# Hybrid encoder layer on one core: the memory queries and the first half of the SSD gate of group one computed in the stage of seven products, the keys of group two one block later

## The chip, the core and the metric

The kernel runs on one core of a Trainium2 chip. TensorE (PE in the profile) multiplies 128x128 stationary tiles by moving tiles of up to 512 columns and writes to PSUM; VectorE (DVE), ScalarE (ACT) and GpSimd (POOL) work beside it, and SyncE (SP) issues the transfers. Each engine takes its own queue in order, and semaphores join them. The metric is the time of one execution in microseconds (us) on the device. Smaller is better.

## The reference

One layer of an encoder for 1280 tokens of width 2048 (256 of a prompt, 1024 of a sample), in fp32:

```python
hn = rms_norm(x, norm_g)
proj = hn @ w_in                       # 2048 -> 4896 columns
xbc, z_ssd, dt_raw, q, k, v, z_att, mq, z_mem = split_cols(proj, IN_SIZES)
xbc = silu(centred_dwconv(xbc))        # 1536 channels, five taps; then a two-way chunked SSD scan (y_f, y_b)
yg = (y_f + y_b + d_skip * xs) * silu(z_ssd)        # 1024 columns; an RMS norm over each half of 512
o_att = window_attention(rms(q), rms(k), v, sink) * silu(z_att)     # 8 heads, window 128
mq = rms_norm(mq.reshape(b, T, 4, 128), mq_norm_g)                  # memory queries, 512 columns
o_mem = softmax(mq @ mk.T * 128 ** -0.5) @ mv * silu(z_mem)         # 256 memory rows
return x + concat([rms(yg), o_att, o_mem]) @ w_out
```

The change touches two pieces of `proj`: the 512 columns `mq` and the first 512 of the 1024 columns `z_ssd` (the gate of the first SSD half). Both are computed for all tokens before and after; what differs is how, for the first half of the tokens.

## The kernel before, in words

**Tokens and precision.** The ten token tiles of 128 form two groups of five, group one (tiles 0 to 4) and group two (5 to 9). x is held turned, features by tokens. Every fp32 product is made of three matmuls on rounded parts: high by high, high by low, low by high. The weights are split on the chip: `wsplit` rounds a 128x512 piece on ACT (`wh`, line 201) and takes the rest on DVE (`wl`, line 202).

**Three forms of a projection block.** `block_tok` (lines 253 to 255) holds the tokens still and streams 512 weight columns: 16 steps of k, five tiles, three matmuls, 240 of 512 columns; its result has tokens on the partitions. `block_feat` (lines 288 to 290) holds 256 weight columns still and streams the tokens in halves of 320; its result is turned, features on the partitions. `block_pair` (lines 1197 to 1199) does a block of two by two (two halves of k, two of 128 columns each, two of 320 tokens) with seven products instead of eight, by Strassen's and Winograd's scheme: a unit covers 256 columns with 8 x 7 x 3 = 168 matmuls of 320 columns, and its result is turned. The sums of weight pieces that it needs are made by `weight_sums` on POOL (four per step of k, line 1169) and split like the weights; the seven accumulators are put together on DVE (`ev_seven`).

**Order of the stages.** Memory keys and values; attention queries of group one; then ten units of seven products for group one (`UNITS`, lines 1506 on): gates of attention and memory, and the convolution channels. Then ordinary blocks: keys, values and dt of group one (`kv`), memory queries (`mq`), the halves of the SSD gate (`z0`, `z1`, and during `z1` the x of group two is loaded). Then group two: five convolution blocks, its `kv`, the sixth convolution block, `q`, attention gate, `z0`, `z1`, `mq`, memory gate; then the output product, with a second stage of seven products at the end.

**Side work.** Attention, memory attention and the SSD scan are generators in two queues (lanes): lane 0 holds key and query preparation, `attn` and `mem_attn`, lane 1 `dt_prep`, `ssd_up`, `ssd_down`. After each k of a block, `pump` takes as many steps from each lane as `RATES` says (for `block_feat` half as many per k), so the rates set how densely side work lies between the block matmuls. `need` forces steps that are required at once. The order within an engine's queue is then fixed when the program is built.

**Side work that the change touches.** `mem_attn(t)` loads a tile of memory queries (line 704), squares it on ACT (707), sums on DVE, takes a reciprocal root on POOL, turns the four heads on PE (715) and splits them, then computes scores, a softmax, and passes the probabilities through a transfer of its own (`mprR`, line 749) to round them for the PE's turn (755). `attn` does the same with `lgR` (648) and `ppt` (658). `ssd_down(t)`, the backward pass of the scan, loads the partial y and the gate of each half (`zd`, line 1011), multiplies them (1031) and squares with a sum (1032). All small PSUM results share a ring of three buffers (`mix`).

**Sums of squares of x.** `x_stats` computes row statistics by ACT squares; for tiles 5, 6 and 7 this happens during the seven-product stage (`stage_stats`), for tiles 8 and 9 as a generator in lane 1.

Of the kernel before, what the change touches and what calls it, by code (L numbers as in the profile page):

```python
# [19 lines left out]
P = 128  # L20
# [22 lines left out]
def hymba_encoder_kernel(  # L43
# [62 lines left out]
    zT_d = [[dram([P, 4, 640], f"zT{c}_{g}") for g in range(2)] for c in range(2)]  # L106
    q_d = [dram([P, 512], f"q_{t}") for t in range(NT)]
    mq_d = [dram([P, 512], f"mq_{t}") for t in range(NT)]
    k_d = [dram([P, P], f"k_{t}") for t in range(NT)]
# [589 lines left out]
    def mem_attn(t):  # L699
# [4 lines left out]
        S.dma_start(q, mq_d[t])  # L704
        yield
        sq = w2("sq")
        A.activation(sq, q, AF.Square)
# [5 lines left out]
        ps = psum("pmq")  # L713
        for h in range(4):
            T.transpose(ps[:, h * P:(h + 1) * P].bitcast(F32R), qr[:, h * P:(h + 1) * P], identr)
# [280 lines left out]
    def ssd_down(t):  # L996
# [8 lines left out]
        for g in range(2):  # L1005
            c = slice(g * 512, (g + 1) * 512)

            y = mp.tile([P, 512], F32, tag="ya" if t % 2 else "rf", name="yd", bufs=2)
            S.dma_start(y, yp_d[t][:, c])
            z = mp.tile([P, 512], F32, tag="xs", name="zd", bufs=2)  # L1010
            S.dma_start(z, z_d[g][t])
# [257 lines left out]
    def ev_seven(kind, f0):  # L1269

        work, o = (conv_left, 2) if kind is None else (gate_left, 0)
# [35 lines left out]
    def gate_left(c, f0, rs):  # L1307
        th = []

        def tanhs():  # L1310
            for r in rs:
                th.append(ev.tile([P, 640], F32, tag="evt", name="th"))
                A.activation(th[-1], r[:, :640], AF.Tanh, scale=0.5)

        def last(i):
            V.scalar_tensor_tensor(out=th[i], in0=th[i], scalar=1.0, in1=rs[i][:, :640], op0=ALU.add, op1=ALU.mult)
            S.dma_start(zT_d[c][0][:, f0 + i, :], th[i])
        return [tanhs, lambda: last(0), lambda: last(1)]
# [27 lines left out]
    def x_stats(grp):  # L1346
        if grp == 0:
            yield from stats([(xrow(t), t) for t in range(5)],
                             lambda i: ev.tile([P, 512], F32, tag="evt" if i % 2 else "evu", name="xst"))
        else:  # L1350
            yield from stats([(xrow(t), t) for t in (8, 9)],
                             lambda i: mp.tile([P, 512], F32, tag="xs" if i % 2 else "ya", name="xst", bufs=2))
# [131 lines left out]
    units = [(i // 2, i % 2 * 2) if i < 4 else (None, 2 * (i - 4)) for i in UNITS]  # L1484
# [44 lines left out]
    queue(1, x_stats, [1])  # L1529
# [30 lines left out]
    for b in range(5):  # L1560
        feat("x", b, ev_conv(1, 2 * b), 1, extra=one_left)
    need(attn, range(4))
    kv_shift()
    run(block_tok(w_kv, 5, ev_dtkv(5)), RATES[1]["kv"], extra=one_left)
# [7 lines left out]

    run(block_tok(w_in_rows("q"), 5, ev_raw(q_d, 5)), RATES[1]["q"], extra=when_done(2, lambda: queue(1, ssd_up, range(4, 8))))
# [108 lines left out]
```

## Time and profile before

| | before |
|---|---|
| median of 3 runs | 1803.69 us (1802.4 to 1804.88) |
| profiled execution | 1804.15 us, of it 1802.4 us span from the first to the last instruction |
| PE busy | 1789.5 us (99%) |
| weight loads busy | 1600.9 us (89%) |
| DVE busy | 1211.0 us (67%) |
| ACT busy | 901.0 us (50%) |
| POOL busy | 457.4 us (25%) |

The times of a matmul in the profile are the time it spends in PE, which overlaps with the next; what a stream costs is seen from start to start, or from a stretch divided by its matmuls. "Idle before" is time in which an engine did nothing, put down to what ended it.

### The profile page before, as it was taken

How to read it: one execution, taken by the hardware profiler on the slowest of the kernel's cores; microseconds unless marked ns; L12 is line 12 of the kernel's file. 1: busy time of each engine (PE TensorE's matmuls, PEld its weight loads, DVE VectorE, ACT ScalarE, POOL GpSimd, SP SyncE). 2: the span in 40 equal slices, each digit the busy share in tenths (PEclk: the TensorE clock that was granted, in tenths of full speed). 3: DMA queues.
4: the chain of work that ended last, by engine and by line, in shares of the span. 5: the costliest groups of instructions: out<-in, count | busy, mean ns of one | idle time of the engine just before them, and what ended most of it. 6: DMA issues, size and time to landing. Idle time of an engine off the chain costs nothing.

```text
span 1802.4 us, 30786 instructions
## 1 busy us (share of the span) xinstructions
PE 1789.5 (99%) x10546; PEld 1600.9 (89%) x10546; DVE 1211.0 (67%) x2303; ACT 901.0 (50%) x1999; POOL 457.4 (25%) x772
## 2 busy tenths in 40 slices
PE   9999999999999999999999999999999999999999
PEld 8789999999887799999989988777888888889999
DVE  5595788877557878775755756556784654766665
ACT  6554455444445757464426645554483533543332
POOL 0105899961010000000000000001100000058775
PEclk9999999999999999999999999999999999999999
DMA  8654454447545655545436556567885664644442
GB/s 298 191 178 123 136 151 147 130 135 217 166 138 173 222 163 156 163 137 154 130 100 202 165 157 194 158 198 243 252 278 179 203 206 144 222 147 147 143 142 79
DMA packets 213293, 309.48 MB, mean 172 GB/s; under 512 B 20560, under 2 KB 92304, under 8 KB 213136
## 3 DMA queue, kind: packets, MB, share of 16 engines
q1 hardware_dynamic: 212992, 307.45, 55.1%
q8 instruction: 83, 1.36, 0.3%
q14 instruction: 74, 0.61, 0.1%
q10 hardware_dynamic: 144, 0.06, 0.0%
HBM read 231.12 MB, written 57.44 MB: 160 GB/s over the span
## 4 chain that ended last, share of the span: by engine, by line
PE 88%; issue 4%; DMA 4%; DVE 2%; ACT 1%; POOL 1%; SPq 0%; ACTq 0%; DVEq 0%; POOLq 0%
PE acc L253 13%; PE acc L255 12%; PE acc L254 12%; PE acc L1199 6%; PE acc L1197 6%; PE acc L1198 6%; PE acc L288 5%; PE acc L289 5%; PE acc L290 5%; PE accm L1198 2%; PE accm L1197 2%; PE accm L1199 2%; PE py L929 2%; PE po L668 1%; PE pmo L770 1%
## 5 line engine op out<-in xcount | busy, mean ns | idle before, releaser
L202 DVE TENSOR_TENSOR wl<-wraw,wh 128x512 fp32r<-128x512 f32 (+1 forms) x480 | 339.4, 709 | 279.4 <-ACT wh L201 271.4
L253 PE MATMUL acc<-wh,xH 128*128 128x512 f32 (+1 forms) x1248 | 480.6, 385 | 0.4 <-DVE dt_all L331 0.4
L254 PE MATMUL acc<-wl,xH 128*128 128x512 f32 (+1 forms) x1248 | 473.5, 379 | 0.9 <-DVE wl L202 0.8
L255 PE MATMUL acc<-wh,xL 128*128 128x512 f32 (+1 forms) x1248 | 472.7, 379 | 0.0
L201 ACT ACTIVATE wh<-wraw 128x512 fp32r<-128x512 f32 (+1 forms) x480 | 292.9, 614 | 355.0 <-PE acc L255 203.0
L253 PEld LDWEIGHTS acc<-wh,xH 128*128 128x128 f32 x1248 | 234.4, 188 | 44.3 <-issue 4.0
L254 PEld LDWEIGHTS acc<-wl,xH 128*128 128x128 f32 x1248 | 234.5, 188 | 44.1 <-DVE wl L202 3.7
L255 PEld LDWEIGHTS acc<-wh,xL 128*128 128x128 f32 x1248 | 234.3, 188 | 44.3 <-issue 1.1
L288 PE MATMUL acc<-xH,wh 128*128 128x320 f32 x640 | 202.8, 317 | 0.0
L289 PE MATMUL acc<-xL,wh 128*128 128x320 f32 x640 | 198.6, 310 | 0.0
L290 PE MATMUL acc<-xH,wl 128*128 128x320 f32 x640 | 198.0, 309 | 0.0
L202 DVE TENSOR_TENSOR sl<-ws,sh 128x384 fp32r<-128x384 f32 x144 | 100.0, 698 | 98.1 <-ACT sh L201 97.8
L201 ACT ACTIVATE sh<-ws 128x384 fp32r<-128x384 f32 x144 | 74.6, 523 | 181.8 <-POOL ws L1169 85.1
L1169 POOL TENSOR_TENSOR ws<-wraw 128x128 f32<-128x128 f32 x144 | 90.8, 631 | 200.3 <-DMA wraw<-in_w_in_pairs_dram 78.2
L289 PEld LDWEIGHTS acc<-xL,wh 128*128 128x128 f32 x640 | 120.2, 188 | 2.8 <-issue 2.4
L288 PEld LDWEIGHTS acc<-xH,wh 128*128 128x128 f32 x640 | 120.2, 188 | 2.2 <-issue 1.6
L290 PEld LDWEIGHTS acc<-xH,wl 128*128 128x128 f32 x640 | 120.2, 188 | 0.3 <-issue 0.2
L628 POOL COPY lg<-nsink 128x2 f32<-128x2 f32 x40 | 11.5, 288 | 412.1 <-DMA lgR<-lg 214.8
L357 DVE SCALAR_TENSOR_TENSOR c<-u,vec,c 128x638 f32<-128x638 f32 (+1 forms) x96 | 89.2, 930 | 12.2 <-ACT c L352 11.8
L1169 POOL TENSOR_TENSOR ws<-ws,wraw 128x128 f32<-128x128 f32 x144 | 96.7, 671 | 0.0
L1169 POOL TENSOR_TENSOR ws<-wraw,ws 128x128 f32<-128x128 f32 x144 | 92.9, 645 | 11.3
L1169 POOL TENSOR_TENSOR wraw<-wraw 128x128 f32<-128x128 f32 x144 | 89.7, 623 | 11.1
(426 smaller groups left out, 3592.1 us busy)
## 6 DMA issues: line engine op xcount, KB each, us to landing
wraw<-in_w_in_laid_dram SPq DMA_DIRECT2D x208, 256.0 KB, 2.9
wraw<-in_w_in_pairs_dram SPq DMA_DIRECT2D x80, 256.0 KB, 2.8
wraw<-in_w_out_laid_dram SPq DMA_DIRECT2D x64, 256.0 KB, 3.2
wraw<-in_w_out_pairs_dram SPq DMA_DIRECT2D x64, 256.0 KB, 2.8
rf<-ac SPq DMA_DIRECT2D x40, 256.0 KB, 3.7
rb<-ac SPq DMA_DIRECT2D x40, 256.0 KB, 4.0
lgR<-lg SPq DMA_DIRECT2D x48, 192.0 KB, 2.2
wraw<-in_w_mem_laid_dram SPq DMA_DIRECT2D x32, 256.0 KB, 4.6
```

The costliest lines, as they stand in the source:

```text
L201: a = A.activation(h, raw, AF.Copy)
L202: b = V.tensor_sub(l, raw, h.bitcast(F32))
L253: T.matmul(ps[t][:, :n], sh, h[:, :n], start=(k_ == 0), stop=False)
L254: T.matmul(ps[t][:, :n], sh, l[:, :n], start=False, stop=False)
L255: T.matmul(ps[t][:, :n], sl, h[:, :n], start=False, stop=(k_ == KT - 1))
L288: T.matmul(o, sh, cur["H", q][:, m, c], start=(k == 0), stop=False)
L289: T.matmul(o, sh, cur["L", q][:, m, c], start=False, stop=False)
L290: T.matmul(o, sl, cur["H", q][:, m, c], start=False, stop=(k == KT - 1))
L1169: G.tensor_tensor(out=o, in0=x, in1=y, op=op)
L1197: T.matmul(ps[p], h, xh, start=(k_ == 0), stop=False)
L1198: T.matmul(ps[p], h, xl, start=False, stop=False)
L1199: T.matmul(ps[p], l, xh, start=False, stop=(k_ == 7))
```

## The change

1. Group one's `mq` and `z0` blocks go. In their place come four units of seven products, so the stage has 14 units instead of 10. Two of them (`y0`, `y1`) make the gate of the first SSD half with the same end as the other gates (tanh and product), stored turned in `yT_d`; two (`m0`, `m1`) store raw memory queries turned in `mT_d`.
2. `mem_attn` of group one reads turned queries. It needs them turned for the scores and by tokens for the sum of squares, so it turns them first, squares what comes out, and splits the loaded tile directly.
3. `ssd_down` of tiles 0 to 4 reads the first half's gate turned, and turns it on PE into a PSUM tile before the product.
4. The sums of squares of tiles 8 and 9 move from lane 1 into the seven-product stage.
5. The keys of group two come after the sixth convolution block instead of before it. `mem_attn` of group one is queued before the `z1` block.
6. The rates are set anew.
7. The weights of the units are laid out for the new order by the host.

```diff
-RATES = ({'kv': (2.14, 1.0), 'mq': (2.57, 1.6), 'z0': (2.35, 1.7), 'z1': (2.35, 1.7)},
-         {'kv': (1.28, 1.5), 'x': (1.87, 1.85), 'q': (1.71, 2.5), 'za': (1.71, 2.5), 'z0': (1.66, 2.6), 'z1': (1.66, 2.65), 'mq': (1.66, 2.8), 'zm': (1.66, 2.85), 'o': (2.09, 1.9)})
+RATES = ({'kv': (2.14, 1.0), 'z1': (3.21, 1.6)},
+         {'kv': (1.5, 1.5), 'x': (2.25, 2.15), 'q': (2.35, 2.5), 'za': (2.19, 2.5), 'z0': (2.14, 2.6), 'z1': (2.03, 2.65), 'mq': (2.03, 2.8), 'zm': (2.03, 2.85), 'o': (2.09, 1.9)})
-UNITS = (0, 4, 1, 5, 2, 6, 7, 3, 8, 9)
+UNITS = (0, 8, 1, 9, 2, 10, 3, 11, 4, 12, 5, 13, 6, 7)
+PAIRS = ('za0', 'za1', 'zm0', 'zm1', 'y0', 'y1', 'm0', 'm1', 'x0', 'x1', 'x2', 'x3', 'x4', 'x5')
...
 def mem_attn(t):
-        S.dma_start(q, mq_d[t])
+        if grp == 0:
+            S.dma_start(hv(q, 4), mT_d[:, :, tc_])
+        else:
+            S.dma_start(q, mq_d[t])
         yield
+        def turned():
+            ps = psum("pmq")
+            for h in range(4):
+                T.transpose(ps[:, h * P:(h + 1) * P].bitcast(F32R), qr[:, h * P:(h + 1) * P], identr)
+            return ps
+        tok_ = turned() if grp == 0 else q
         sq = w2("sq")
-        A.activation(sq, q, AF.Square)
+        A.activation(sq, tok_, AF.Square)
...
-        ps = psum("pmq")
-        for h in range(4):
-            T.transpose(ps[:, h * P:(h + 1) * P].bitcast(F32R), qr[:, h * P:(h + 1) * P], identr)
+        feat_ = q if grp == 0 else turned()
-        A.activation(qh, ps, AF.Copy)
+        A.activation(qh, feat_, AF.Copy)
-        V.tensor_sub(ql, ps, qh.bitcast(F32))
+        V.tensor_sub(ql, feat_, qh.bitcast(F32))
...
 def ssd_down(t):
+            if g == 0 and t < 5:
+                z = mp.tile([P, 512], F32R, tag="xs", name="zd", bufs=2)
+                S.dma_start(hv(z.bitcast(F32), 4), yT_d[:, :, tok])
...
+            if g == 0 and t < 5:
+                zr, z = z, psum("pz")
+                for j in range(4):
+                    T.transpose(z[:, j * P:(j + 1) * P].bitcast(F32R), zr[:, j * P:(j + 1) * P], identr)
...
-        yield from stats([(mrow(i), 10 + i) for i in range(4)] + [(xrow(t), t) for t in (5, 6, 7)],
+        yield from stats([(mrow(i), 10 + i) for i in range(4)] + [(xrow(t), t) for t in range(5, 10)],
...
+    def turned_left(dst, f0, rs):
+        def store():
+            for i in range(2):
+                S.dma_start(dst[:, f0 + i, :], rs[i][:, :640])
+        return [store]
...
-    queue(1, x_stats, [1])
...
-    run(block_tok(w_in_rows("mq"), 5, ev_raw(mq_d, 0)), RATES[0]["mq"],
+    queue(0, mem_attn, range(5))
+    run(block_tok(w_in_rows("z1"), 5, ev_gate(1, 0)), RATES[0]["z1"], refill_x(1),
         extra=when_done(1, lambda: queue(1, ssd_up, range(4))))
-    queue(0, mem_attn, range(5))
-    tok("z0", w_in_rows("z0"), ev_gate(0, 0))
-    tok("z1", w_in_rows("z1"), ev_gate(1, 0), refill_x(1))
...
-    for b in range(5):
+    for b in range(6):
         feat("x", b, ev_conv(1, 2 * b), 1, extra=one_left)
...
     run(block_tok(w_kv, 5, ev_dtkv(5)), RATES[1]["kv"], ...)
...
-    feat("x", 5, ev_conv(1, 10), 1, extra=one_left)
```

More of the change, by code (lines that the diff above doesn't have):

```diff
@@ L1344, in stats, with x_stats @@
                 yield
[L1346 to L1352, printed above, removed]
+    def x_stats(_):
+        yield from stats([(xrow(t), t) for t in range(5)],
+                         lambda i: ev.tile([P, 512], F32, tag="evt" if i % 2 else "evu", name="xst"))
     def stage_stats():
-        yield from stats([(mrow(i), 10 + i) for i in range(4)] + [(xrow(t), t) for t in (5, 6, 7)],
+        yield from stats([(mrow(i), 10 + i) for i in range(4)] + [(xrow(t), t) for t in range(5, 10)],
                          lambda i: fin.tile([P, 512], F32, tag="xst", name="sst"), ahead=1, group=3)
@@ L1482, in hymba_encoder_kernel @@
         extra=lambda k: p_step(16 + k))
-    units = [(i // 2, i % 2 * 2) if i < 4 else (None, 2 * (i - 4)) for i in UNITS]
+    dests = (zT_d[0][0], zT_d[1][0], yT_d, mT_d)
+    units = [(dests[i // 2], i % 2 * 2) if i < 8 else (None, 2 * (i - 8)) for i in UNITS]
     squares = stage_stats()
@@ L1558, in one_left, with gate @@
             some_left()
-    for b in range(5):
+    for b in range(6):
         feat("x", b, ev_conv(1, 2 * b), 1, extra=one_left)
+    def gate(name, c, after=None):
+        for b in range(2):
+            feat(name, b, ev_gateT(c, 1, 2 * b), 1, after if b else None)
     need(attn, range(4))
     kv_shift()
-    run(block_tok(w_kv, 5, ev_dtkv(5)), RATES[1]["kv"], extra=one_left)
+    run(block_tok(w_kv, 5, ev_dtkv(5)), RATES[1]["kv"], extra=lambda k: some_left() if left else None)
     queue(0, k_prep, range(5, 10))
@@ L1567, in hymba_encoder_kernel @@
     queue(1, dt_prep, [5])
-    feat("x", 5, ev_conv(1, 10), 1, extra=one_left)
-    def gate(name, c, after=None):
-        for b in range(2):
-            feat(name, b, ev_gateT(c, 1, 2 * b), 1, after if b else None)
     run(block_tok(w_in_rows("q"), 5, ev_raw(q_d, 5)), RATES[1]["q"], extra=when_done(2, lambda: queue(1, ssd_up, range(4, 8))))
@@ L1653 @@
     at = {n: c for n, c, _ in _blocks()}
[L1654 to L1656 removed]
+    at.update({f"{n}{b}": at[s][256 * b:256 * b + 256] for n, s in (('y', 'z0'), ('m', 'mq')) for b in range(2)})
+    c = _np.concatenate([at[PAIRS[i]] for i in UNITS])
+    p = w[:, c].reshape(2, 8, P, len(UNITS), 2, P)
+    inputs['w_in_pairs'] = _np.stack([p[0, :, :, :, 0], p[1, :, :, :, 0], p[1, :, :, :, 1], p[0, :, :, :, 1]]).transpose(3, 1, 2, 0, 4).reshape(len(UNITS), 8, P, 512)
     inputs['w_mem_laid'] = _np.asarray(inputs['w_mem_kv'])[0].reshape(KT, P, 2, 512).transpose(2, 0, 1, 3)
```

16 lines of the change are left out of this document (8 added, 8 removed).

## The prediction, made before the result was known

> **What bounds the kernel now.** I read the page's first and fourth parts, then busy times by stretch, then PE's waits, and last single tiles.
>
> ```profile
> PE 1789.5 (99%) x10546; PEld 1600.9 (89%) x10546; DVE 1211.0 (67%) x2303; ACT 901.0 (50%) x1999; POOL 457.4 (25%) x772
> ...
> PE 88%; issue 4%; DMA 4%; DVE 2%; ACT 1%; POOL 1%; SPq 0%; ACTq 0%; DVEq 0%; POOLq 0%
> ```
>
> PE is busy for all but 13 us of the 1802.4 us span, and the chain that ended last is PE for 88%. Time can be won only by taking work off PE, and lost only by making PE wait. The stretches are stages: seven products for group one (151.9 to 399.2), keys, values and dt of group one up to 430.8, memory queries (to 491.5), first half of the SSD gate (to 554.7), second half (to 632.6), five convolution blocks and the keys of group two (to 862.8), its other projections (to 1257.2), the memory gate and the output blocks, of which the last (from 1545.8) is matmuls alone. Columns: stretch, length, then busy time and instructions of PE, PEld (weight loads), DVE, ACT and POOL, the clock, the DMA share and GB/s.
>
> ```profile
> core 0: us, PE busy (x) PEld busy (x) DVE busy (x) ACT busy (x) POOL busy (x), PEclk, DMA share, GB/s
> 151.90:399.20 247.30, 246.64 (x1682) 245.56 (x1682) 198.05 (x298) 126.34 (x253) 204.82 (x310) 1.00 0.47 138
> ...
> 430.80:491.50 60.70, 60.34 (x293) 50.11 (x293) 40.02 (x87) 20.88 (x44) 6.15 (x10) 1.00 0.51 162
> 491.50:554.70 63.20, 63.20 (x316) 52.87 (x314) 34.49 (x74) 32.49 (x86) 5.96 (x11) 1.00 0.50 153
> 554.70:632.60 77.90, 77.87 (x408) 61.37 (x405) 66.76 (x139) 52.66 (x129) 7.42 (x14) 1.00 0.63 201
> 632.60:862.80 230.20, 229.62 (x1643) 220.96 (x1642) 162.43 (x349) 127.65 (x305) 13.05 (x19) 1.00 0.51 156
> ...
> 1545.80:1600.40 54.60, 54.60 (x241) 44.99 (x241) 36.80 (x61) 24.75 (x42) 9.21 (x16) 1.00 0.56 172
> ```
>
> The last row prices an ordinary block: 54.60 / 241 = 0.227 us from one 512-column matmul to the next. The first row prices a unit of seven products: ten units of 168 matmuls of 320 columns in 247.3 us, 24.7 us each, 0.147 us from start to start. PE is full in both, at a granted clock of 1.00.
>
> What PE waited for between the two stages of seven products:
>
> ```profile
> engine line waited for: us in total, times, longest us
> PE ppt L658 <- DMA lgR<-lg: 2.4, 2, 1.4
> PE psc L634 <- ACT pT L659: 1.5, 2, 0.9
> PE pmt L755 <- DVE c L357: 0.6, 1, 0.6
> PE pmo L770 <- ACT mpT L759: 0.5, 1, 0.5
> PE acc L253 <- DVE dt_all L331: 0.4, 1, 0.4
> PE pr L991 <- ACT so L993: 0.2, 1, 0.2
> ```
>
> Together 5.6 us in 1201 us. The largest are turns of attention probabilities (ppt) that stand in PE's queue before their transfer (lgR) has landed.
>
> **The change, part by part.**
>
> Removed: two ordinary blocks of group one (memory queries, first half of the SSD gate), each 16 x 5 x 3 = 240 matmuls of 512 columns: 2 x 240 x 0.227 = 109.0 us of PE. Their stretches hold 60.7 + 63.2 = 123.9 us; the other 14.9 us are side work laid between the matmuls, which is not removed but moves on.
>
> Added: four units, 4 x 24.7 = 98.9 us of PE. Net -10.1 us. Seven matmuls for eight would by columns alone save 13.6 us; 320 columns carry the same fixed part per matmul as 512, and that takes the rest.
>
> The units' cover: per unit DVE is busy 198.05 / 10 = 19.8 us, POOL (the weight sums) 20.5, ACT 12.6, against PE's 24.7. The memory-query units only store, so they are lighter than these. The sums of squares of two more token tiles come into this stage, eight ACT pieces with their loads and two short POOL pairs, over twelve units: the ACT and POOL shares hide them. Leftovers of a stall: PE's waits in this stage were
>
> ```profile
> PE acc L1199 <- DVE wl L202: 0.7, 2, 0.5
> ```
>
> so 0.07 us per unit; for four more +0.3 us (bounds 0, and 4 x 0.5 = 2.0 if each new unit meets the longest one).
>
> Transposes: the stored gate is now features by tokens, so the backward SSD step turns four 128x128 pieces in each of five tiles: 20 more on PE. The memory queries still have four per tile; for group one they come before the square instead of after it. The nearest row has four such transposes of the same type between block matmuls:
>
> ```profile
> 733.83 0.31 PE L290 MATMUL acc<-xH,wl 128*128 128x320 f32 x1
> 733.98 0.46 PE L715 MATMUL pmq<-identr,mq 128*128 128x128 f32 x4
> 734.27 0.38 PE L288 MATMUL acc<-xH,wh 128*128 128x320 f32 x1
> 734.49 0.31 PE L289 MATMUL acc<-xL,wh 128*128 128x320 f32 x1
> ```
>
> From 733.98 to 734.27 the four take 0.29 us, and the next matmul 0.22 instead of 0.147: 0.36 us per tile, 5 x 0.36 = +1.8 us. [...]
>
> The turned gate takes one of three PSUM buffers until ACT has squared the product. The nearest row for a full PSUM ring is psc waiting on ACT pT, 1.5 us in two: 0 to 5 x 0.75 = 3.8 us. I take 0, as the other 18 such steps of two halves show no wait of this sort, and keep 3.8 for the range.
>
> The memory query of group one is now turned one step behind its load, where it was two steps behind:
>
> ```profile
> L715 PE MATMUL pmq<-identr,mq x40: 221/245/624, 734.0 to 1486.9; 128*128 128x128 f32 x40
> ...
> L704 SPq DMA_DIRECT2D mq<-mq x10: 320/478/608, 716.2 to 1475.4; - x10
> ...
> DMA to landing us min/median/max: 2.0/3.4/4.7
> ```
>
> The first load was issued 17.8 us ahead of its transposes and the last 11.5; a step of some 2.5 us less leaves the slowest landing (4.7) covered. I take 0; the upper end is 5 x 1.2 = 6 us, with the mean wait on a transfer, 1.2 us, from the list of waits. Behind such a transpose the block matmuls of the step would wait, as PE takes its queue in order.
>
> DMAs: the weights are as many bytes, in as many transfers of 256 KB; ten stores of 128x512 become eight of 128x640. SP's queue gets three instructions fewer in all, POOL 128 more sums, all within the seven-product stage.
>
> Side work: two ordinary blocks fewer means 32 fewer places between matmuls for the attention, SSD and memory steps of group one. The keys of group two come one convolution block later, and the steps per matmul group rise: in the convolution blocks from 1.87 to 2.25, with the query block from 1.71 to 2.35, in the gate blocks from 1.66 to 2.14 and 2.03. In the two built programs, priced by start-to-start times of this trace, a turn of probabilities stands a median 9.9 us of PE work behind its scores before and 8.7 after; of the 60 turns (40 windowed, 20 memory) 7 stood within 7 us and 13 do after. These 7 went with the 2.4 and the 0.6 us of the list, 0.43 each; six more give +2.6 us. Bounds: -1 us (fewer steps now stand in the dense stretch before 632.6) and the second rival below.
>
> DVE in the denser stretch: of its 74.5 us in the two removed blocks, weight halves are
>
> ```profile
> 430.80:554.70 123.90, 22.26 (x33) 1.00 0.51 158
> ```
>
> and the gate products
>
> ```profile
> L304 DVE SCALAR_TENSOR_TENSOR zs<-zs,acc 128x512 f32<-128x512 f32 x20 | 13.7, 685 | 8.5 <-ACT zs L303 8.5
> ```
>
> five of them, 3.4 us, which go with the blocks; 48.8 us move on. If all of it fell between 554.7 and 862.8, DVE would be busy 66.8 + 162.4 + 48.8 = 278 of 308 us, 90%. Between 554.7 and 632.6 it was busy 86% and PE idle 0.03 us. I take nothing for it.
>
> Sum: -10.1 + 0.3 + 1.8 + 2.6 = -5.4 us. The profiled execution took 1804.15 us (span 1802.4 and 1.75 around it), 0.5 above the median of 1803.69: 1798.75 for such an execution, 1798.3 us beside the median.
>
> **The rivals.**
>
> First, the gain is eaten by waits. If PE's 5.6 us double because every chain of side work has a fifth less PE work to hide behind, the sum is -10.1 + 0.3 + 1.8 + 5.6 = -2.4: 1801.3 us, not to be told from no change (a measurement of this kernel tells about 0.2%, 3.6 us). For it: turns wait already. Against it: most of the distances that shrink were far above what a chain needs.
>
> Second, slower: the turns of probabilities become the bound of the dense stages. Each chain is scores, reductions on DVE, exponentials on ACT, scaling on DVE, then a transfer, and PE stands still at the turn when it is late, as here:
>
> ```profile
> 1263.36 0.31 PE L290 MATMUL acc<-xH,wl 128*128 128x320 f32 x1
> 1264.69 0.62 PE L658 MATMUL ppt<-identr,lgR 128*128 128x128 f32 x4 [1.02 <-DMA lgR<-lg]
> ```
>
> Price 1.2 us each. The place is the convolution blocks and the query block of group two. It cancels -8.0 from the seventh further waiting turn on, and is slower by over 0.2% from the tenth. Were 15 of the 60 to wait, 13 more than now: -8.0 + 15.6 = +7.6, 1811 us. For it: DVE and ACT are busier there, so the chains lengthen while the distances shrink. Against it: from 554.7 to 632.6 steps stood as densely, with no wait of PE over its 77.9 us.
>
> Third, the change doesn't do what it says: the new units are bound by weight loads rather than matmuls. PEld is busy 245.56 of 247.3 us there, 99%, against 82% in the ordinary block, and a load's slice is
>
> ```profile
> L1198 PEld LDWEIGHTS accm<-tL,wh x160: 187/188/189, 154.2 to 398.7; 128*128 128x128 f32 x160
> ```
>
> At 188 ns for each of 672 loads the units would take 126.3 us: -109.0 + 126.3 + 1.8 + 2.6 = +21.7, 1825 us. Against it stands the measured 0.147 us from start to start; slices overlap. [...]
>
> **How the numbers follow.** The forecast (faster by more than 0.2%, 1794 to 1800) has 0.63, the first rival 0.23, the second 0.13, the third 0.01. So faster 0.63, same 0.23, slower 0.14. The low end 1794 is -10.1 + 1.8 - 1 = -9.3 with no further wait. The high end 1808 takes in the first rival with either bound (the PSUM ring's 3.8 or the queries' 6.0) and the second up to ten or eleven further waiting turns; some 0.06 lie above it and 0.06 below the low end. The forecast's own range is 1794 to 1800.
>
> **What would show it.** Right: fourteen units of 24.7 us each, some 346 us; the second half of the gate straight after the keys; a list of PE's waits of 7 to 10 us; five groups of four pz transposes at 0.3 us. Wrong: units above 25.5 us with waits on wl (cover of DVE or POOL lost); PE waiting on lgR, mprR or mq in the convolution, key and query blocks of group two for 10 us or more; or acc waiting on wl there, which would make DVE the bound.

## The result: slower by 0.17%, where 0.3% faster was forecast

| | before | changed |
|---|---|---|
| median of 20 executions each, on one chip | 1805.14 us (1802.4 to 1807.79) | 1807.89 us (1803.4 to 1811.52) |
| ratio, 95% interval | | 1.0017 [1.0010, 1.0024] |
| profiled execution | 1804.15 us, span 1802.4 | 1809.46 us, span 1807.7 |
| idle time of PE up to its last matmul, profiled execution | 9.2 us | 15.6 us |
| time at half clock before the last 5 us, profiled execution | 0 | 17.1 us |
| loss by the clock (span times one minus the mean granted clock), mean of 20 | 0.8 us (the executions taken beside e1 below) | 4.8 us |

By the bound of 0.2% that the prediction set this is no change that can be told; the interval lies above 1. The forecast was 1798.3 us. The page of the changed kernel, first and fourth parts:

```profile
PE 1788.3 (99%) x10758; PEld 1618.1 (90%) x10758; DVE 1250.6 (69%) x2358; ACT 913.4 (51%) x2029; POOL 539.3 (30%) x900
...
PE 87%; issue 5%; DMA 4%; DVE 2%; ACT 1%; POOL 1%; SPq 0%; ACTq 0%; POOLq 0%; DVEq 0%
```

The shares hardly differ from those of before, so the answer is not in them. Busy times of PE by stretch say more (columns: stretch, length, PE's busy time and instructions, granted clock, DMA share, GB/s):

```profile
core 0: us, PE busy (x), PEclk, DMA share, GB/s
150.40:495.70 345.30, 344.65 (x2353) 1.00 0.47 141
528.50:596.80 68.30, 64.53 (x293) 0.95 0.63 191
596.80:635.30 38.50, 35.80 (x238) 0.91 0.48 145
635.30:836.90 201.60, 201.39 (x1399) 1.00 0.51 155
566.50:573.30 6.80, 5.67 (x22) 0.50 0.74 201
600.60:607.40 6.80, 6.27 (x25) 0.50 0.36 118
1498.30:1501.70 3.40, 3.20 (x11) 0.50 0.23 86
```

The first row is the stage of seven products: fourteen units in 345.3 us, 24.7 us each, as forecast. The next two are the second gate block of group one and the first convolution block of group two. PE stands idle there for 3.8 and 2.7 us, where the gate block of before had 0.03 us, and the mean clock is below 1. The last three rows are the stretches in which the granted clock was 0.50; the kernel before has none of them ahead of its end. A 512-column matmul takes twice its spacing there, 0.43 us against 0.227:

```profile
569.36 0.63 PE L256 MATMUL acc<-wh,xH 128*128 128x512 f32 x1
569.79 0.63 PE L257 MATMUL acc<-wl,xH 128*128 128x512 f32 x1
```

What PE waited for:

```profile
engine line waited for: us in total, times, longest us
PE pmt L767 <- DMA mprR<-mpr: 4.2, 4, 2.4
PE pmk L446 <- issue: 3.4, 1, 3.4
PE pk L503 <- ACT kh L495: 2.7, 1, 2.7
PE pst L867 <- ACT fh L881: 0.8, 2, 0.4
...
PE acc L1219 <- DVE wl L205: 0.3, 1, 0.3
```

The two largest single waits are new lines that the prediction had not named: the turn of a memory key (pmk) in the second gate block and the turn of a key (pk) in the block behind it. The first, in order of time over all engines:

```profile
561.79 0.72 ACT L434 ACTIVATE sq<-mkr,rx 128x512 f32<-128x512 f32 x1 [1.24 <-DMA mkr<-mr]
...
565.17 0.75 DVE L440 SCALAR_TENSOR_TENSOR mkr<-mkr,rx,r 128x512 f32<-128x512 f32 x1 [1.18 <-POOL r L123]
566.84 0.69 DVE L441 TENSOR_TENSOR mkr<-mkr,state 128x512 f32<-128x512 f32 x1
...
567.62 1.09 PE L446 MATMUL pmk<-identr,mkr 128*128 128x128 f32 x4 [3.39 <-issue]
```

From the square to the end of the last product on DVE the chain takes 5.7 us, no longer than for the same key in the kernel before (6.4). What differs is when PE comes to the turn. This is the fourth memory key, and the loads of the four are

```profile
L428 SPq DMA_DIRECT2D mkr<-mr x4: 383/426/561, 518.5 to 556.7; - x4
...
DMA to landing us min/median/max: 2.7/2.9/5.0
```

The fourth was issued at 556.7 and took the 5.0 us. The chain, counted from the issue of the load, was through after 10.8 us; PE was at the turn after 7.5 (564.2) and stood for 3.39. For the other three keys of this kernel PE came 17 to 26 us after the load, and for the fourth key of the kernel before 16.5 us after it, with a chain of 12.0. The mean rate alone doesn't give this away. At 3.21 steps for each of 16 k in a block of 68.3 us a step is 68.3 / (16 x 3.21) = 1.3 us, and the four steps from the square to the turn are 5.3; before, in the memory-query block, 60.7 us at 2.57 steps made 1.5 us a step and 5.9 for four. Both are less than the chain, and only one kernel waits: `pump` takes the steps of one k together, and PE was at the turn 2.4 us behind the start of the square here and 10.8 us behind it there, 4.4 us after the last product. In the kernel before:

```profile
470.68 0.69 DVE L438 TENSOR_TENSOR mkr<-mkr,state 128x512 f32<-128x512 f32 x1
...
475.80 0.60 PE L443 MATMUL pmk<-identr,mkr 128*128 128x128 f32 x4
```

The second wait of the changed kernel:

```profile
599.57 0.60 ACT L306 ACTIVATE zs<-acc 128x512 f32<-128x512 f32 x1 [2.68 <-DMA z<-zs]
...
600.58 0.50 ACT L495 ACTIVATE kh<-kr 128x128 fp32r<-128x128 f32 x2
...
601.13 0.49 PE L503 MATMUL pk<-identr,kh 128*128 128x128 f32 x2 [2.69 <-ACT kh L495]
```

ACT stood for 2.68 us ahead of a piece of the gate's end, whose tile was still being stored; behind it in ACT's queue stood the rounding of a key, and for that PE stood in the next block.

The sum over the two profiled executions: -8.3 us of matmuls, +6.4 of PE idle, and +7.6 for the half clock (half of the 15.14 us that PE was busy in it): +5.7, against spans that differ by 5.3. In the medians of 20 the clock's part is smaller, +4.0 (4.8 less 0.8), so that some +7 are left for waits and the total is +2.8.

### The profile page after: what moved, and what is told of

Read it like the earlier page. It is cut to its first block, busy times and chain, and to the rows that moved or that the text cites. A ratio compares the mean times of both kernels' runs of the same rounds, so it can differ in the third digit from the quotient of the medians.

```text
span 1807.7 us, 31532 instructions
## 1 busy us (share of the span) xinstructions
PE 1788.3 (99%) x10758; PEld 1618.1 (90%) x10758; DVE 1250.6 (69%) x2358; ACT 913.4 (51%) x2029; POOL 539.3 (30%) x900
## 4 chain that ended last, share of the span: by engine, by line
PE 87%; issue 5%; DMA 4%; DVE 2%; ACT 1%; POOL 1%; SPq 0%; ACTq 0%; POOLq 0%; DVEq 0%
PE acc L256 10%; PE acc L257 9%; PE acc L258 9%; PE acc L1219 7%; PE acc L1217 7%; PE acc L1218 7%; PE acc L291 5%; PE acc L292 5%; PE acc L293 5%; PE accm L1218 3%; PE accm L1217 3%; PE accm L1219 3%; PE py L941 2%; PE po L671 1%; PE pmo L782 1%
## 5 line engine op out<-in xcount | busy, mean ns | idle before, releaser
L256 PE MATMUL acc<-wh,xH 128*128 128x512 f32 (+1 forms) x1088 | 418.5, 385 | 0.1
L257 PE MATMUL acc<-wl,xH 128*128 128x512 f32 (+1 forms) x1088 | 412.0, 379 | 0.4 <-DVE wl L205 0.4
L258 PE MATMUL acc<-wh,xL 128*128 128x512 f32 (+1 forms) x1088 | 411.8, 379 | 0.0
L256 PEld LDWEIGHTS acc<-wh,xH 128*128 128x128 f32 x1088 | 205.0, 188 | 37.4 <-issue 3.9
L258 PEld LDWEIGHTS acc<-wh,xL 128*128 128x128 f32 x1088 | 205.0, 188 | 37.2 <-issue 0.5
L257 PEld LDWEIGHTS acc<-wl,xH 128*128 128x128 f32 x1088 | 205.4, 189 | 36.5 <-DVE wl L205 2.2
L205 DVE TENSOR_TENSOR sl<-ws,sh 128x384 fp32r<-128x384 f32 x176 | 124.3, 709 | 104.6 <-ACT sh L204 102.1
L1189 POOL TENSOR_TENSOR ws<-wraw,ws 128x128 f32<-128x128 f32 x176 | 116.4, 661 | 13.8
L1189 POOL TENSOR_TENSOR ws<-ws,wraw 128x128 f32<-128x128 f32 x176 | 117.4, 667 | 0.0
L1189 POOL TENSOR_TENSOR wraw<-wraw 128x128 f32<-128x128 f32 x176 | 111.9, 636 | 13.7
```

Of the source, the lines that this page charges most:

```text
L205: b = V.tensor_sub(l, raw, h.bitcast(F32))
L256: T.matmul(ps[t][:, :n], sh, h[:, :n], start=(k_ == 0), stop=False)
L257: T.matmul(ps[t][:, :n], sh, l[:, :n], start=False, stop=False)
L258: T.matmul(ps[t][:, :n], sl, h[:, :n], start=False, stop=(k_ == KT - 1))
L1189: G.tensor_tensor(out=o, in0=x, in1=y, op=op)
```

## The experiments

Two theories. **A**: the second gate block of group one carries side work that was spread over three blocks; its preparation of memory keys and keys is late there, and the stand-stills halve the clock. **B**, the prediction's second rival: the turns of probabilities wait for their transfers (lgR, mprR) wherever side work is denser. Times are medians, in us; each ratio is against the kernel before on the same chip.

| | edit | us | ratio [95%] |
|---|---|---|---|
| changed | | 1807.9 | 1.0017 [1.0010, 1.0024] |
| e1 | changed, `z1` rate 2.35 and 1.2 | 1801.1 | 0.9984 [0.9975, 0.9993] |
| e2 | changed, early start, `z1` 2.68 and 1.35 | 1810.2 | 1.0025 [1.0015, 1.0035] |
| e3 | changed, group two's rates of before | 1826.9 | 1.0118 [1.0103, 1.0132] |
| e4 | before, with stand-stills put in | 1816.2 | 1.0062 [1.0049, 1.0075] |
| e5 | before, no transfer of probabilities | 1799.3 | 0.9975 [0.9965, 0.9986] |
| e6 | changed, no transfer of probabilities | 1804.7 | 1.0005 [0.9997, 1.0014] |
| e7 | e1 and e6 together | 1794.9 | 0.9945 [0.9933, 0.9957] |
| e8 | only the gate half moved | 1801.6 | 0.9987 [0.9977, 0.9997] |
| e9 | e2 and e6 together | 1799.5 | 0.9975 [0.9966, 0.9983] |
| e10 | e7, keys of group two not later | 1801.1 | 0.9982 [0.9973, 0.9991] |
| e11 | only the memory queries moved | 1804.6 | 1.0004 [0.9995, 1.0012] |
| e12 | changed, narrow filler in two waits | 1811.8 | 1.0046 [1.0032, 1.0061] |
| e13 | changed, wide filler | 1806.3 | 1.0022 [1.0011, 1.0033] |
| e14 | changed, again | 1806.5 | 1.0022 [1.0011, 1.0033] |

### e1: the second gate block's rate

```diff
-RATES = ({'kv': (2.14, 1.0), 'z1': (3.21, 1.6)},
+RATES = ({'kv': (2.14, 1.0), 'z1': (2.35, 1.2)},
```

> The changed kernel with one pair of rates set back: in the second half of the SSD gate lane 0 takes 2.35 steps per k instead of 3.21 and lane 1 1.2 instead of 1.6; some 14 steps of lane 0 and 6 of lane 1 come later. Theory A (memory-key and key preparation stands too densely in that block; PE stands still for 3.4 and 2.7 us at their turns and the granted clock then halves for 6.8 us each): no gap of PE above 1.5 us between 520 and 620 us, no half clock there, that block and the first convolution block 7 to 10 us shorter together; a span of 1799 to 1802 us, ratio to the kernel before 0.996 to 0.999. Theory B (the turns of probabilities in the denser blocks of group two eat the gain): these blocks do not change or get longer, ratio 1.001 or above.

The two waits are gone, and so is the half clock; the list of PE's waits, and the block's stretch with the place where the changed kernel ran at half clock:

```profile
PE acc L291 <- DVE zs L307: 2.0, 3, 0.9
PE pmt L767 <- DMA mprR<-mpr: 1.4, 2, 1.1
...
PE ppt L661 <- DMA lgR<-lg: 1.0, 2, 0.6
```

```profile
528.50:588.30 59.80, 59.80 (x288) 1.00 0.63 197
566.50:573.30 6.80, 6.80 (x32) 1.00 0.71 258
```

The block is 59.8 us instead of 68.3, with no idle time of PE; part of that is side work that moved on. PE now comes to the fourth memory key's turn 13.4 us after the load (7.5 in the changed kernel), which is enough although the load took 6.4 us this time. Two numbers of one line turn 0.17% slower into 0.16% faster, so A's place is right.

### e2 and e3: the same steps elsewhere

e2 gives the block its room in another way: the side work starts four steps earlier, in the key block.

```diff
-RATES = ({'kv': (2.14, 1.0), 'z1': (3.21, 1.6)},
+RATES = ({'kv': (2.14, 1.0), 'z1': (2.68, 1.35)},
...
-    run(block_tok(w_kv, 5, ev_dtkv(0), ...), RATES[0]["kv"], hold=5,
+    run(block_tok(w_kv, 5, ev_dtkv(0), ...), RATES[0]["kv"], hold=1,
```

> The changed kernel with the side work begun earlier: from the second k of the key block of group one instead of the sixth (some 9 steps of lane 0 and 4 of lane 1), and the rates in the second half of the gate cut by as many (2.68 and 1.35). Later blocks keep their rates and hold the same steps. Theory A: the gaps at the memory keys' and keys' turns go or fall below 1.5 us, no half clock there, ratio 0.996 to 0.999. Theory B: the later blocks are unchanged, so ratio 1.001 or above.

The stand-stills of the gate block went, and the time did not come: new ones stood at mprR (2.60 us, with half clock behind it, and 2.34; mean granted clock 0.999). The profiled execution was the fastest of the nine (1804.6 us, the median is 1810.2), so its trace doesn't show all that was lost. That was a miss for A as the only cause; e9 takes it up.

e3 puts the rates of group two back to those of before, in the changed kernel:

```diff
-         {'kv': (1.5, 1.5), 'x': (2.25, 2.15), 'q': (2.35, 2.5), 'za': (2.19, 2.5), ...
+         {'kv': (1.28, 1.5), 'x': (1.87, 1.85), 'q': (1.71, 2.5), 'za': (1.71, 2.5), ...
```

> The changed kernel with the rates of all blocks of group two as in the kernel before (1.87 instead of 2.25 in the convolution blocks, 1.71 instead of 2.35 in the query block and so on), the gate block still at 3.21. More steps are left for the output blocks. Theory A: the gaps and the half clock near 565 and 600 us stay, and the time stays or rises, ratio 1.001 to 1.006. Theory B: the blocks from the second convolution block to the memory gate get 5 us or more shorter than their PE work explains, ratio below 1.000.

```profile
PE acc L256 <- DVE yt L408: 12.2, 1, 12.2
PE pmk L446 <- issue: 3.6, 1, 3.6
PE psc L637 <- ACT pT L662: 3.4, 1, 3.4
PE ppt L661 <- DMA lgR<-lg: 3.2, 2, 2.5
```

The wait on the memory key stays, as A has it, but the time rose further than either theory had it. The steps that no longer fit are forced at the end: 12.2 us, then 13.7 us of half clock. The denser side work of group two is what two removed blocks make necessary, and no mistake in itself.

### e4: does a stand-still halve the clock?

In the kernel before, a chain of POOL steps (3, 4 and 5 of them) is put in front of the end of the first tile of three output blocks; it adds zero to the result.

```diff
+STILL = {0: 3, 512: 4, 1024: 5}
...
+            if t == 0 and c0 in STILL:
+                g = sm.tile([P, 8], F32, tag="still", name="still", bufs=1)
+                A.activation(g, ps[:, :8], AF.Square)
+                for _ in range(STILL[c0]):
+                    G.tensor_tensor(out=g, in0=g, in1=mhalf[:, :8], op=ALU.pow)
+                G.tensor_tensor(out=g, in0=g, in1=g, op=ALU.subtract)
+                V.tensor_add(yt[:, :8], yt[:, :8], g)
```

> The kernel before, with PE made to stand still at the start of the second, third and fourth output blocks: the evacuation of the first tile is put behind a chain of 3, 4 and 5 slow POOL steps of some 1.7 us, which compute nothing that is kept. Expected stand-stills of PE some 2, 3.5 and 5 us. If a stand-still of some 2.4 us or more halves the granted clock afterwards (as the changed kernel's trace has it behind 3.4, 2.7 and 2.4 us), the second and third are followed by 3.4 to 6.8 us at half clock, and each costs its own length and another 1.7 to 3.4 us; in all some 10 us of gaps and 5 to 7 us of clock, ratio 1.007 to 1.010. If the clock has another cause, it stays at 1.00 and the ratio is 1.004 to 1.006.

One chain was hidden; two made PE stand for 2.63 and 6.43 us. Stretches of this trace:

```profile
1334.10:1337.50 3.40, 1.72 (x13) 1.00 0.99 346
1337.50:1340.90 3.40, 3.40 (x13) 0.50 1.00 329
1549.10:1552.50 3.40, 0.00 (x0) 1.00 0.00 0
1552.60:1559.40 6.80, 3.91 (x9) 0.50 0.46 138
```

The 6.43 us brought 6.8 us of half clock. A gap of 1.73 us that the kernel made by itself (first two rows) brought 3.4 us of it, and the 2.63 us brought none (granted clock 1.00 from 1482.60 to 1490.00 us). So length alone does not decide; the section on the hardware says what the traces show of it. The ratio, 1.0062, lies between the two cases of the expectation.

### e5, e6, e7: without the transfers

VectorE writes the scaled probabilities straight into the rounded tile that PE turns; the same for lgR in `attn`. e5 is this edit on the kernel before, e6 on the changed one, e7 on e1.

```diff
+            st_[hp] = mp.tile([P, 512], F32R, tag="wa", name="mprR", bufs=WA)
             for j in range(2):
-                V.tensor_scalar(out=pr[:, c], in0=pr[:, c], scalar1=den[:, j:j + 1], scalar2=0.5,
+                V.tensor_scalar(out=st_[hp][:, c], in0=pr[:, c], scalar1=den[:, j:j + 1], scalar2=0.5,
-            st_[hp] = mp.tile([P, 512], F32R, tag="wa", name="mprR", bufs=WA)
-            S.dma_start(st_[hp].bitcast(F32), pr)
```

> The kernel before, with the probabilities written by VectorE straight into the tiles that TensorE turns (lgR, mprR), so that the 48 + 40 transfers between them fall away; nothing else. Theory A (what the change lost, it lost to the dense preparation of keys and memory keys in the second gate block of group one and to the clock that halves after the stand-stills): before has no such stand-still, so little is to be had here: 1801 to 1805, ratio 0.999 to 1.0005. Theory B (the turns of probabilities wait for their transfers wherever the side work is dense): before is at its rate's limit only seldom (0.2 to 2.4 us a line in the list of waits), so 1800 to 1803, ratio 0.998 to 0.9995. This run is the base line of the next one.

> The changed kernel with the same edit: probabilities straight into lgR and mprR, no transfer. Theory A: the waits of 3.4 us on the memory keys and 2.7 us on the keys stay, with two stretches of half clock of 6.8 us (6.8 us lost) behind them in most executions; only the 4.2 us at mprR and their half clock go. 1803 to 1806, ratio 0.9995 to 1.001 against before, and 0 to 3 us over the run e5. Theory B: the waits that ate the 8.4 us of TensorE work stand at the transfers, so all of it comes back: 1795 to 1799, ratio 0.995 to 0.9975, 5 to 8 us under e5.

> The changed kernel with the probabilities written directly and the rate of the second gate block of group one at 2.35 and 1.2 steps instead of 3.21 and 1.6 (the edit of e1). Theory A: as e1, with the waits at mprR gone as well: 1798 to 1800, ratio 0.996 to 0.998; e7 lies 4 to 7 us under e6. Theory B: the rate of that block adds nothing once the transfers are gone: within 2 us of e6. If both causes hold, e7 is the fastest of all, 1795 to 1797.

The waits of e6, then of e7:

```profile
PE pmk L446 <- issue: 3.4, 1, 3.4
PE pk L503 <- ACT kh L495: 2.4, 1, 2.4
```

```profile
PE acc L291 <- DVE zs L307: 1.6, 3, 0.7
```

e5 came out 1.7 us under the lower end of A's range and just under that of B. e6 keeps the two waits at the memory key and the key and is 0.05% over before: B alone explains the smaller part. It is also 5.4 us over e5, more than A's own forecast of 0 to 3. e7 has neither sort of wait, no half clock (mean 1.000), and is the fastest of all, 0.55% under before. The two edits do more together than apart: by the ratios the rate brings 6.0 us with transfers (changed to e1) and 10.8 without (e6 to e7), a difference of 4.8 where the four intervals together leave some 3.4 open; the transfers cost 4.5 us in the kernel before, 2.2 in the changed one, 7.0 in e1. With both edits the change is worth 4.4 us (e7 against e5, both without transfers; 5.4 by the ratios). That is near the -5.4 us of the forecast, but not for its reason: the transfers whose waits it priced are gone from both, and up to the last matmul PE is idle for 7.7 us in e7 and 4.4 in e5.

### e8, e11: half of the change each

Twelve units instead of fourteen; the other stage stays an ordinary block ahead of the second gate block, with the latter's old rate, and group two between the old and the new rates. e8 moves the gate half, e11 the memory queries. From e8's edit:

```diff
-UNITS = (0, 8, 1, 9, 2, 10, 3, 11, 4, 12, 5, 13, 6, 7)
-PAIRS = ('za0', 'za1', 'zm0', 'zm1', 'y0', 'y1', 'm0', 'm1', 'x0', 'x1', 'x2', 'x3', 'x4', 'x5')
+UNITS = (0, 6, 1, 7, 2, 8, 3, 9, 4, 10, 5, 11)
+PAIRS = ('za0', 'za1', 'zm0', 'zm1', 'y0', 'y1', 'x0', 'x1', 'x2', 'x3', 'x4', 'x5')
...
+    run(block_tok(w_in_rows("mq"), 5, ev_raw(mq_d, 0)), RATES[0]["mq"],
+        extra=when_done(1, lambda: queue(1, ssd_up, range(4))))
     queue(0, mem_attn, range(5))
-    run(block_tok(w_in_rows("z1"), 5, ev_gate(1, 0)), RATES[0]["z1"], refill_x(1),
-        extra=when_done(1, lambda: queue(1, ssd_up, range(4))))
+    tok("z1", w_in_rows("z1"), ev_gate(1, 0), refill_x(1))
```

> Half of the change: the gate half of group one goes into the stage of pairs (twelve units), the memory queries stay an ordinary block ahead of the second gate block, which keeps the rates of before (2.35, 1.7); the blocks of group two run at rates between those of before and after (1.89 to 2.13). By its TensorE work it is half way, -4.2 us. Theory A: the dense block is thinned out again, so no wait over 1.5 us on keys and memory keys, no half clock: 1799 to 1801, ratio 0.9975 to 0.9985. Theory B: half of the denser side work's price stays with half of the gain: 1804 to 1806, ratio 1.000 to 1.001.

> The other half of the change: the memory queries of group one go into the stage of pairs, the gate half stays an ordinary block ahead of the second gate block, which keeps the rates of before (2.35, 1.7); transfers as in the changed kernel, rates of group two as in e8. By its TensorE work half way too, -4.2 us. Theory A: with the dense block thinned out, as e8: 1799 to 1803, ratio 0.9975 to 0.9995, with no wait over 1.7 us on keys or memory keys. If the turned memory queries themselves cost time (turns ahead of the sum of squares, a longer chain), it is 2 us or more over e8, and the waits stand at pmq, pms or psc of the memory.

In both, the waits at the memory key and the key are gone, and mprR is the largest line (first e8, then e11):

```profile
PE pmt L764 <- DMA mprR<-mpr: 4.5, 2, 2.9
```

```profile
PE pmt L767 <- DMA mprR<-mpr: 4.8, 2, 2.9
```

The gate half brings 0.13%, just short of what A gave; the memory queries bring nothing, and e11 is 3 us over e8, where A had much the same time for both. Their lists of waits differ by tenths, the clock accounts for 0.9 us (a mean loss of 2.3 us against 1.4), and the rest is open. That the turns ahead of the squares cost it isn't borne out by the list: neither pmq nor pms stands among its first lines.

### e9, e10: what e2 left open, and the later keys

e9 is e2's edit on e6. e10 is e7 with the key block of group two back ahead of the sixth convolution block:

```diff
-    for b in range(6):
+    for b in range(5):
         feat("x", b, ev_conv(1, 2 * b), 1, extra=one_left)
...
+    feat("x", 5, ev_conv(1, 10), 1, extra=one_left)
```

> The edit of e2 (the side work starts at step 1 instead of 5 of group one's key block, the second gate block at 2.68 and 1.35 steps) on the changed kernel whose probabilities go directly into lgR and mprR (e6). It is for what e2 left open: its profiled execution showed waits on mprR of 2.60 and 2.34 us, each near the size that halves the clock, and its other executions were 3 to 7 us longer. If those executions lost their time to turns that wait for transfers (theory B as a second cause), e9 has none of them: 1795 to 1799, a spread like that of e7, 6 us or more under e6. If the early start itself loses the time (the side work of the key block, the block ahead of it), e9 stays 6 to 10 us over e7: 1801 to 1805.

> The third part of the change undone in the fastest kernel (e7): the key block of group two goes back ahead of the sixth convolution block. The same instructions in another order. Theory A gives this part no share: within 1.5 us of e7, 1793.5 to 1796.5. If the later keys cost time (less side work ahead, so that it is denser after), e10 is 2 us or more faster than e7; if they were what makes the denser side work possible, e10 waits for convolution rows or on steps that come too early and is 2 us or more slower.

e9 came out between its two cases: 0.50% under e2, so that most of e2's loss was at the transfers, but 4.6 us over e7, so that the early start has a price too. e10 is 6.2 us over e7, where A had given the later keys no share. Its list:

```profile
PE pmo L779 <- ACT mpT L768: 2.6, 1, 2.6
PE acc L291 <- DVE zs L307: 2.2, 2, 1.6
...
PE pq L619 <- DVE qh L614: 1.2, 1, 1.2
```

The first is followed by 6.8 us of half clock and lies in group two. The longer of the second, 1.6 us with 3.4 us of half clock behind it, stands at the first matmul behind the second gate block; the order on every engine is the same in the traces of e7 and e10 up to 769 us, so this wait is no effect of the edit but a difference between executions. The clock accounts for 2.6 of the 6.2 us (a mean loss of 2.6 us against 0.0). So without the later keys the change brings nothing even here (e10 is 1.8 us over e5, on another chip, and e7 4.4 us under it); by which step they bring it isn't shown.

### e12, e13, e14: the price of the half clock by itself

Products that nobody reads ahead of the two late turns, 30 and 24 of 128 columns (e12) or 8 and 6 of 512 (e13); e14 is the changed kernel again.

From e13's edit:

```diff
         ps = psum("pmk")
+        if i == 3:
+            for _ in range(8):
+                T.matmul(ps, identr, mkH[:, 0:2, :], start=True, stop=True)
...
         ps = psum("pk")
+        if t == 2:
+            for _ in range(6):
+                T.matmul(ps, identr, mkH[:, 0:2, :], start=True, stop=True)
```

> The changed kernel, its rates and transfers untouched, with work on TensorE that nobody reads inside its two waits of the second gate block: 30 products of 128 columns of the unit matrix ahead of the turn of the fourth memory key, 24 ahead of the turn of the third key (1.6 to 2.0 us each by the 58 to 87 ns of a turn of 128 columns), written to the bank that the turn then overwrites. It parts the price of the half clock from the price of the waits. If the clock halves because TensorE stands still for 2.2 us of a stretch of 3.4 us, the half clock at 566 and 600 us goes while both waits stay as long (filled for the most part): the loss by the clock falls from 4.8 us in the mean to 1 to 2 us, and the time to 1803 to 1805, 3 to 5 us under the changed kernel. If the half clock costs nothing beside the waits, or comes from something else than the standing, 1807 to 1810: the same or the filler on top.

> As e12, but the filler is of 8 products of 512 columns ahead of the turn of the fourth memory key and 6 ahead of the turn of the third key (1.8 and 1.4 us by the spacing of 0.227 us). Counted in columns over stretches of 3.41 us, the windows at 563 and 597 us of the changed kernel streamed the array for 0.94 and 0.97 us, and all windows of the fourteen traces that were followed by half clock stayed under 1.28 us; with the filler they reach 2.6 and 2.2 us. If that count is what halves the clock, no half clock stands at 566 and 600 us, the loss by the clock falls from 4.8 to 1 or 2 us, and the time lies 2 to 4 us under e14. If the half clock comes from the late turn and not from the empty array, it stays, and e13 is level with e14 or up to 2 us over it.

> The changed kernel as it is, for e13 to be compared with on one chip: 1806 to 1809, ratio 1.001 to 1.0025; half clocks of 6.8 us at 566 and 600 us, in the same places as in the first profile, since the waits there come from the order of the work and not from chance.

e14 shows the two waits (3.4 and 1.8 us) in the same places, each with 3.4 us of half clock behind it this time (mean granted clock 0.998). e13 didn't do what it was built for. PE's order in its trace:

```profile
562.26 2.03 PE L447 MATMUL pmk<-mkH,identr 128*128 128x512 f32 x8
564.13 0.40 PE L256 MATMUL acc<-wh,xH 128*128 128x512 f32 x1
564.37 0.40 PE L257 MATMUL acc<-wl,xH 128*128 128x512 f32 x1
568.23 0.69 PE L449 MATMUL pmk<-identr,mkr 128*128 128x128 f32 x2 [3.46 <-DVE mkr L441]
```

```profile
597.00:604.00 7.00, 7.00 (x45) 1.00 0.68 222
```

The order of PE's queue is set with the cost of the filler in it, and eight matmuls of the block now stand behind the turn: the filler took the place of work and not of the wait, which stayed at 3.46 us with its half clock (0.51 granted from 567.60 to 571.00 us). At the second place it did fill the wait; PE was busy for all of 597 to 604 us and the clock stayed at 1.00 where e14 has 3.4 us of half clock. In all, 3.2 us of filler cost nothing (e13 is 0.2 us under e14), which fits a saving of that size but doesn't show it. e12's filler ran some 112 ns apart, 6 us in all. Ten matmuls of the block moved behind the first turn in the same way, 1.47 us of the wait were left, and the half clock at 569 us stayed (0.50 granted from 569.24 to 572.65); the one behind the second turn went. The kernel is 4 to 5 us slower than the changed one by the ratios. So the half clock's price stands on the clocks of the profiles alone, and no run has parted it from the waits.

## Why the prediction was wrong, point by point

- **Removed and added TensorE work** (-109.0, +98.9): right. Fourteen units took 345.3 us where 346 was given. From start to start, waits left out, the matmuls of 512 columns add up to 110.3 us less in e1 than in the kernel before, those of 320 columns to 99.9 us more. The part of a matmul that does not go with its columns, which the prediction took as equal for both lengths, is some 14 ns in the trace of the kernel before: medians of 0.227, 0.147 and 0.133 us from start to start at 512, 320 and 288 columns, 0.417 ns for each column.
- **Pair-stage waits** (+0.3): right; the row acc L1219 on wl has 0.3 us in all, less than half of before.
- **Transposes of the gate** (+1.8): right. The twenty take 1.6 us from start to start and stand without any wait:

```profile
L1044 PE MATMUL pz<-identr,zd x20: 223/250/252, 1238.3 to 1304.7; 128*128 128x128 f32 x20
```

- **PSUM ring and memory-query load** (0 and 0): right; no wait on mq or pz is in the list.
- **DVE in the denser stretch** (0): right as to DVE. It was taken from busy shares, though, and the chain that was late there runs through a load, ACT, DVE, POOL and DVE with steps between.
- **Side work, +2.6: the step that failed.** It priced the denser side work by turns of probabilities alone, at 0.43 us each, and had the stretch before 632.6 as a place of gain (the bound of -1), since "fewer steps now stand in the dense stretch". That looked at the number of steps and not at the rate: in the second gate block it went from 2.35 to 3.21 steps per k, the largest jump in the diff, and the chains there are those of memory keys and keys. The distance in PE's queue between a chain and its turn, which the prediction worked out for probabilities, it did not work out for these. What the runs showed in its place: 6.1 us of waits at two turns in that block and the next, with half clock behind them; taking the rate back is worth 6 us (e1) to 11 us (e7 against e6).
- **No term for the clock.** The clock was read as 1.00 throughout and left out. In the changed kernel's trace 6.8 us at 0.50 follow a gap of 3.39 us, so a stand-still there cost more than its length; in e4 a gap of 1.73 us, beside short products, was followed by 3.4 us at 0.50.
- **First rival** (waits double, 1801.3): the nearest in mechanism: it gave the waits +5.6 us, and PE's idle time went up by 6.4. The clock's 4 us it did not have.
- **Second rival** (turns of probabilities bound the dense stages, 1811): nearest in time, and a second cause in fact (e5, e6, e7, e9), but with four waiting memory turns (4.2 us) and not with fifteen. The sign that the prediction named for itself being wrong, 10 us of waits on lgR, mprR or mq, did not come up; it was wrong in another place.

## What to carry to other kernels

When blocks are removed that carried side work, look first at the block in which the displaced preparation now runs, and at every chain in it. For each, take from the built program or the trace how much PE work stands between the issue of the chain's load and the turn that needs it, and compare this with the chain's own length, the load included (here 7.5 us against 10.8). The mean time of a step is too coarse for it. A wait of PE of 2 to 3.4 us is to be priced with the half clock that may follow: 1.7 to 3.4 us more at the three such waits of the changed kernel, as read from the clocks. And a change that takes work off the bound engine pays only when its rates are set anew with it: the same change was 0.17% slower, 0.16% faster with two numbers altered, and 0.55% faster than before when the probabilities' transfers went as well, of which the transfers alone bring 0.25% in the kernel before (e5).

## What the runs showed of the hardware

In the profiled execution of the changed kernel the granted clock was 0.50 from 566.48, 600.61 and 1498.32 us on, for 6.83, 6.83 and 3.41 us. The starts lie 34.13 and 897.71 us apart, 10 and 263 times 3.413 us. In e4 such stretches lasted 3.4 and 6.8 us, in e3 one lasted 13.7. What sets these lengths isn't shown. The windows ahead of the first two half clocks of the changed kernel, and the emptiest one of the kernel before ahead of its last 5 us, which was not followed by half clock:

```profile
563.10:566.50 3.40, 1.13 (x5) 1.00 0.96 334
597.20:600.60 3.40, 1.24 (x9) 1.00 0.76 257
```

```profile
1343.70:1347.10 3.40, 2.00 (x11) 1.00 0.97 337
```

What sets the windows ahead of a half clock apart in these two traces is how long columns stream in them, counted at 0.417 ns a column ((0.227 - 0.147) / 192 us, from the spacings at 512 and 320 columns) in windows of 3.41 us laid from a half clock's start. The three ahead of the half clocks of the changed kernel streamed for 0.94, 0.97 and 1.00 us, the one ahead of the half clock in the last 5 us of the kernel before for 0.76; all other whole windows at full clock from the eighth us on, which were not followed by half clock, streamed for at least 1.47 us. Idle time alone sorts the windows less well: e12's filler of 128 columns was 112 ns apart for an estimated 53 ns of streaming (128 x 0.417), and its window from 565.82 us on, with 1.47 us of idle time and such filler (1.03 us streamed), was followed by 3.4 us of half clock, while the window of the changed kernel from 1802.11 us on, with 1.63 us of idle time (1.47 streamed), was not. How products of 64 and 128 columns weigh isn't settled by this count. The same wait cost differently from one execution to the next: the wait at the memory key, 3.39 us in the first trace of the changed kernel and 3.41 in e14, was followed by 6.8 us of half clock in the one and by 3.4 in the other. This is part of why the changed kernel spreads over 8 us (1803.4 at a mean clock of 1.000, 1811.5 at 0.996) and the kernel before over 5.
